# Layered diffusion block on one Trainium2 core: the 31-tap convolution of the conformer's second 128 channels moved from VectorE to TensorE

## The chip, the core and the metric

The kernel runs on one core of one Trainium2 chip. The metric is the device time of one execution in microseconds (us), as the median of several runs. TensorE is called PE here, its weight loads PEld, VectorE DVE, ScalarE ACT, GpSimd POOL; SP is the queue that issues nearly all transfers (DMAs).

## The reference, cut to what matters

There are two layers over 1024 latent and 256 context tokens, 1024 wide. In each layer a normalised stream `h` is projected by `w_in`, four mixers of 256 channels work on parts of the projection, and their outputs go through `w_out` and then a mixture of experts. The third mixer is the conformer:

```
def conformer_conv(pc, conv_w, conv_b, ln_g, ln_b, w_pw, b_pw):
    u = pc[..., :W_C] * jax.nn.sigmoid(pc[..., W_C:])
    u = dwconv(u, conv_w, conv_b, (CONF_K // 2, CONF_K // 2))
    u = layer_norm(u, ln_g, ln_b)
    return jax.nn.silu(u) @ w_pw + b_pw
```

`dwconv` is a depthwise convolution: each of the 256 channels has 31 taps of its own, and runs along the tokens. Latent and context tokens are convolved apart. In the second layer the context produces no mixer output, so the conformer has 1024 tokens there and 1280 in the first.

## The kernel before, in words

A layer runs in four stages: the projection (`phase1`, L2049), the attention inside the same function, a stage that holds the Hyena mixer and the conformer (in `run`, from L2180 on), and the output projection with the experts. Instructions are traced in the order of the code; a planner then lays them out on each engine by readiness and by that order, so that work traced late fills gaps of the engine, and each engine runs its own list strictly in order.

In the projection, `win` (L1070) loads 128 columns of `w_in` at a time, splits them into two parts of reduced precision (ACT at L974, POOL or DVE at L977) and runs three matmul sets at L1091 for every group of 512 or 256 tokens; `win_v` does the like at L1133. Between these blocks lies the recurrence `rglru` (L1403): for each of two channel blocks there are six steps (three stretches, two directions). In a step POOL starts `rg_u` (L1428), three DVE instructions finish it (L1430), PE multiplies it by the gate weights (L1433), and ACT, DVE and POOL go on from there. There is one `rg_u` buffer, so the next step starts only when L1440 of this one is done.

The conformer's input is written by `glu_evac` (L1137): ACT takes a tanh, DVE multiplies at L1147 into the padded row buffer `cu`, one per 128 channels. `conv31` (L1470) is traced at the end of the projection for both channel blocks. It is one DVE instruction at L1475 and 30 at L1477 per block, each over all tokens of the layer (1295 or 1024 elements per partition), accumulating in `cacc`, which is then stored to `cd` in DRAM.

In the later stage `hyena_in` (L1739) loads a row block `hx`, runs L1753 on POOL and two L1756 on DVE, and PE turns the result with matmuls at L1763. `hyena` is a generator: its first part is pulled by `next(hy)`, the rest is traced after the conformer. The long convolution of the Hyena mixer is the matmuls at L1800. `conformer` (L1490) loads the convolved channels back (`cx`, L1499) for 512, 512 and 256 tokens, forms the layer norm through PE (L1502, L1511, L1486), and ends with the product L1524. All of these take PSUM buffers `rg`, of which there are three.

Of the kernel before, what the change touches and what calls it, by code (L numbers as in the profile page):

```python
# [238 lines left out]
FT = mybir.dt.float32  # L239
# [3 lines left out]
AF = mybir.ActivationFunctionType  # L243
OP = mybir.AluOpType
AX = mybir.AxisListType
SP = mybir.EngineType.SP
D = 1024
P = 128
# [629 lines left out]
TL, TC = 1024, 256  # L878
T0 = TL + TC
C8 = math.sqrt(0.5)  # L880
GROUPS = [(0, 512, 0), (512, 512, 0), (1024, 256, 1)]


# [9 lines left out]
class Kern:  # L893
# [22 lines left out]
    def setup(self):  # L916
        nc, I = self.nc, self.I
        moe_consts(self, NFIX)
        c = self.consts
        self.eps = c.tile([P, 2], FT, name="eps")  # L920
        nc.vector.memset(self.eps[:, 0:1], 1e-6)
        nc.vector.memset(self.eps[:, 1:2], 1e-5)
        self.modd = self.dram.tile([2, 2, 6 * D], FT, name="modd")
        self.xd = self.dram.tile([TL, D], FT, name="xd")
        self.x1d = [self.dram.tile([T0 if l == 0 else TL, D], FT, name=f"x1d{l}") for l in range(2)]
        self.pd = self.dram.tile([6 * P, T0], FT, name="pd")
        self.qkd = self.dram.tile([2, 8, 32, 4, T0], FT, name="qkd")
        self.hd = [self.dram.tile([17, P, 512], FT, name=f"hd{l}") for l in range(2)]
        self.hdc = self.dram.tile([5, P, 512], FT, name="hdc")
        self.h2d = [self.dram.tile([T0 if l == 0 else TL, D], FT, name=f"h2d{l}") for l in range(2)]  # L930

        self.fd = [self.dram.tile([2 * T0, D], FT, name="fd0"), self.x1d[1]]
        self.lst = self.dram.tile([64 * P, 4], I32, name="lst")
        self.yd = self.dram.tile([8, P, T0], FT, name="yd")
        self.cd = self.dram.tile([2 * P, T0 + 15], FT, name="cd")

    def params(self, l, psum, R):

# [198 lines left out]
    def glu_evac(self, w, u):  # L1137

        nc, th = self.nc, []

        def f(p, t0, n, v):
            th[:] = [w.tile([P, 512], FT, name="stg", bufs=2)]
            nc.scalar.activation(th[0][:, :n], p[:, :n], AF.Tanh, scale=0.5)

        def g(p, t0, n, v):
            o = t0 + 15 + (15 if v else 0)
            nc.vector.scalar_tensor_tensor(u[:, o:o + n], th[0][:, :n], 1.0, p[:, :n], op0=OP.add, op1=OP.mult)  # L1147
        return f, g

    def d_evac(self, w, row):  # L1150
# [316 lines left out]
        return f  # L1467


    def conv31(self, l, w, b, u, ctx_out):  # L1470
        nc = self.nc
        N = TL + (15 + TC if ctx_out else 0)
        a = w.tile([P, N], FT, name="cacc")
        cw = lambda j: self.cw[:, j * 2 + b:j * 2 + b + 1]
        nc.vector.tensor_scalar(a, u[:, 0:N], cw(0), self.pc("c_conv_b", b), op0=OP.mult, op1=OP.add)  # L1475
        for j in range(1, 31):
            nc.vector.scalar_tensor_tensor(a, u[:, j:j + N], cw(j), a, op0=OP.mult, op1=OP.add)  # L1477
        nc.sync.dma_start(self.cd[b * P:(b + 1) * P, :N], a)

    def spread(self, p, r, t):  # L1480

# [5 lines left out]
        return p  # L1487


    def conformer(self, l, w, ctx_out):  # L1490
        nc, I = self.nc, self.I
        om = w.tile([P, P], FT, name="om", bufs=1)
        nc.vector.memset(om, 1.0 / 256)
        wpw = w.tile([P, 2, 256], FT, name="wpw", bufs=1)
        nc.sync.dma_start(wpw, I["c_w_pw"][l].rearrange("(k p) f -> p k f", p=P))
        for o, t0, n in ((0, 0, 512), (512, 512, 512), (15 + TL, TL, TC))[:3 if ctx_out else 2]:
            acc = w.tile([P, 2, 512], FT, name="cx", bufs=2)
            for b in range(2):
                nc.sync.dma_start(acc[:, b, :n], self.cd[b * P:(b + 1) * P, o:o + n])  # L1499
            pm = self.pr.tile([P, 512], FT, name="rg")  # L1500
            for b in range(2):
                nc.tensor.matmul(pm[:, :n], om, acc[:, b, :n], start=(b == 0), stop=(b == 1))  # L1502
            sq = w.tile([P, 2, 512], FT, name="csq", bufs=1)
            for b in range(2):
                nc.vector.tensor_tensor(acc[:, b, :n], acc[:, b, :n], pm[:, :n], op=OP.subtract)
            nc.scalar.activation(sq[:, :, :n], acc[:, :, :n], AF.Square)

            pv = self.pr.tile([P, 512], FT, name="rg")
            for q in range(n // P):
                for b in range(2):  # L1510
                    nc.tensor.matmul(pv[:, q:q + 1], sq[:, b, q * P:(q + 1) * P], om[:, 0:1], start=(b == 0),  # L1511
                                     stop=(b == 1))
            r = w.tile([P, 4], FT, name="crs", bufs=2)[:, :n // P]
            nc.scalar.activation(r, pv[:, :n // P], AF.Sqrt, bias=self.eps[:, 1:2])
            nc.vector.reciprocal(r, r)
            r = self.spread(self.pr.tile([P, 512], FT, name="rg"), r, w.tile([P, 512], FT, name="cr", bufs=1))
            for b in range(2):
                nc.vector.tensor_tensor(acc[:, b, :n], acc[:, b, :n], r[:, :n], op=OP.mult)
                nc.scalar.activation(acc[:, b, :n], acc[:, b, :n], AF.Silu, scale=self.pc("c_ln_g", b),
                                     bias=self.pc("c_ln_b", b))  # L1520
            for m in range(2):
                p = self.pr.tile([P, 512], FT, name="rg")
                for b in range(2):
                    nc.tensor.matmul(p[:, :n], wpw[:, b, m * P:(m + 1) * P], acc[:, b, :n], start=(b == 0),  # L1524
                                     stop=(b == 1))
                t = w.tile([P, 512], FT, name="cy", bufs=2)
                nc.scalar.activation(t[:, :n], p[:, :n], AF.Identity, bias=self.pc("c_b_pw", m))
                nc.sync.dma_start(self.yd[4 + m, :, t0:t0 + n], t[:, :n])


    def sin_layer(self, w, p, r, n, f, fb, out):
# [517 lines left out]
    def phase1(self, l, ctx_out, top, p1, hs, ahead, done):  # L2049
# [5 lines left out]
        with p1 as c:  # L2055
            with ExitStack() as c2:
# [9 lines left out]
                vt = self.pool(c, "vt").tile([P, 10, 256], FT, name="vt")  # L2066
                wd = self.pool(c, "wd")

                self.cw = self.keep.tile([P, 62], FT, name="cw")
                a = self.col["c_conv_w"]  # L2070
                nc.vector.tensor_scalar(self.cw, self.pp[:, a:a + 62], 0.5, None, op0=OP.mult)
                N = TL + 30 + (15 + TC if ctx_out else 0)
                us = []
                self.pr = self.pool(c2, "r_ps", 3, space=PSUM)
                with ExitStack() as c3:
                    rg = self.pool(c3, "rgl")
# [8 lines left out]
                    def gate(b, h):  # L2085
                        self.win(l, w, [2 + b], hs, allg, [self.rglru_out(wd, b, h)])
                    h = recur(0)
                    for b in range(2):
                        u = wd.tile([P, N], FT, name="cu", bufs=2)
                        nc.gpsimd.memset(u[:, 0:15], 0.0)  # L2090
                        nc.gpsimd.memset(u[:, 15 + TL:30 + TL], 0.0)
                        if ctx_out:
                            nc.gpsimd.memset(u[:, N - 15:N], 0.0)
                        self.win(l, w, [12 + b, 10 + b], hs, allg, self.glu_evac(wd, u))
                        us.append(u)
                    gate(0, h)
                    h = recur(1)
                    with ExitStack() as c4:
# [6 lines left out]
                            if i == 0:  # L2105
                                self.win_v(l, w, wq, hs, vt)
                        gate(1, h)
                for b in range(2):
                    self.conv31(l, wd, b, us[b], ctx_out)
            yt = self.pool(top, f"yt{l}", side="right").tile([P, nblk, 256], FT, name="yt")  # L2110

            def rest(rows):
# [20 lines left out]
    def run(self):  # L2133
# [30 lines left out]
        for l in range(2):  # L2164
# [16 lines left out]
            with ExitStack() as c:  # L2181
                self.pm = self.pool(c, "x_ps", 5, space=PSUM)
                self.pr = self.pool(c, "r_ps", 3, space=PSUM)
                ut = self.pool(top, f"ut{l}", side="right").tile([P, nblk, 768], FT, name="ut")
                hy = self.hyena(l, self.pool(top, f"hy{l}", side="right"), ctx_out, ut, yt)
                with ExitStack() as c2:
                    hc = self.pool(c2, "hc")
                    w = self.pool(c2, "xy")
                    for b in range(2):
                        self.hyena_in(l, hc, b, ut, ctx_out)  # L2190
                    next(hy)
                    self.to_channels(w, yt, 1, nblk)
                    for b in range(2, 6):
                        self.hyena_in(l, hc, b, ut, ctx_out)
                    self.conformer(l, w, ctx_out)
                wop = ExitStack()
                wo = self.pool(wop, "wo")
                with ExitStack() as c2:
                    wo = self.out_weights(l, wo, self.pool(c2, "wor"))
                pin = self.inputs(self.pool(wop, "pi"))  # L2200
                for _ in hy:
                    pass
# [136 lines left out]
```

## Time and profile before

| what | us |
|---|---|
| median of 3 runs (lowest, highest) | 3560.05 (3556.44, 3561.93) |
| the profiled execution's own time | 3566.47 |
| its span, first to last instruction | 3564.7 |
| PE busy, DVE busy in it | 3079.1, 2283.5 |
| the 120 instructions at L1477 | 194.7 |

The span is the profiled execution from its first to its last instruction; 1.8 us of its own time lie around it. Busy times are shares of the whole span and mix stages with different limits, so the rows further down are read stage by stage. A group's mean is over all instructions of that form. Matmul records are pipelined: the time from one start to the next is the pace, and the printed duration is longer. One fp32 matmul of the code is two records.

### The profile page before, as it was taken

To read this page: it belongs to the slowest core of one execution; us is meant where nothing else is said; L and a number is where in the kernel's file an instruction comes from. 1 tells how busy PE (TensorE), PEld (TensorE's weight loads), DVE (VectorE), ACT (ScalarE), POOL (GpSimd) and SP (SyncE) were. 2 spreads that over 40 slices of the span, in tenths; PEclk is the share of its full clock that TensorE was granted. 3 is DMA by queue.
4 is the path that set the end of the run, shared out by engine and by line. 5 is a ranking of instruction groups with operands and counts; after the bars stand their busy time and mean duration, and the time that the engine had idled before them with its cause. 6 is when DMAs were issued, how large, how long until landed. Compare 5 with 4: busy or idle time off the path is not lost. (4 is left out here: it accounts for less than half of the span.)

```text
span 3564.7 us, 43773 instructions
## 1 busy us (share of the span) xinstructions
PE 3079.1 (86%) x14952; PEld 2075.7 (58%) x14952; DVE 2283.5 (64%) x3339; ACT 1539.3 (43%) x2497; POOL 722.9 (20%) x573
## 2 busy tenths in 40 slices
PE   5898888997889699999998487799788799889995
PEld 1246665776678354677555466667667665456563
DVE  6674885787768434475544679578876764347644
ACT  4234344773324233465544354367433343235433
POOL 2213452003210101110110435400230112111110
PEclk8899899998999699999999698989989799999998
DMA  6752226215555888986878512312446389978897
GB/s 189 227 193 62 69 87 215 72 38 178 166 190 195 261 307 320 357 320 237 317 259 333 195 33 101 128 41 70 157 149 228 130 297 361 373 260 280 268 335 252
DMA packets 414223, 734.95 MB, mean 206 GB/s; under 512 B 46725, under 2 KB 181746, under 8 KB 413994
## 3 DMA queue, kind: packets, MB, share of 16 engines
q1 hardware_dynamic: 395242, 694.30, 56.3%
q0 software_dynamic: 18752, 37.80, 3.8%
q8 instruction: 119, 1.95, 0.2%
q14 instruction: 110, 0.90, 0.1%
HBM read 647.75 MB, written 105.30 MB: 211 GB/s over the span
## 5 line engine op out<-in xcount | busy, mean ns | idle before, releaser
L688 DVE TENSOR_TENSOR wl<-wr,wh 128x1024 fp32r<-128x1024 f32 (+1 forms) x440 | 516.0, 1203 | 344.6 <-ACT wh L687 335.7
L687 ACT ACTIVATE wh<-wr 128x1024 fp32r<-128x1024 f32 (+1 forms) x440 | 442.7, 1038 | 391.9 <-PE mm L739 228.7
L743 PE MATMUL mm<-wr,xl 128*64 128x512 f32 x1216 | 329.6, 610 | 6.2 <-DMA wr<-in_moe_w_gate_dram 3.2
L1091 PE MATMUL mm<-hh,wih 128*128 128x512 f32 (+1 forms) x752 | 290.5, 387 | 10.6 <-ACT stg L1155 7.0
L1091 PE MATMUL mm<-hh,wil 128*128 128x512 f32 (+1 forms) x752 | 289.6, 386 | 10.5 <-POOL wil L977 9.9
L1091 PE MATMUL mm<-hl,wih 128*128 128x512 f32 (+1 forms) x752 | 290.9, 387 | 4.4 <-DVE hl L977 3.8
L739 PE MATMUL mm<-wh,xh 128*128 128x512 f32 x704 | 289.6, 413 | 5.1 <-ACT wh L687 4.5
L739 PE MATMUL mm<-wl,xh 128*128 128x512 f32 x704 | 280.0, 398 | 8.4 <-DVE wl L688 8.3
L739 PE MATMUL mm<-wh,xl 128*128 128x512 f32 x704 | 278.6, 397 | 0.0
L1477 DVE SCALAR_TENSOR_TENSOR cacc<-cu,cw,cacc 128x1295 f32<-128x1295 f32 (+1 forms) x120 | 194.7, 1623 | 1.9
L739 PEld LDWEIGHTS mm<-wh,xh 128*128 128x128 f32 x704 | 134.0, 190 | 90.8 <-issue 47.5
L680 POOL DMA_INDIRECT gb<-h2d,ridx x82 | 100.5, 1225 | 420.0 <-PE tr L707 175.9
L1225 DVE TENSOR_REDUCE m<-A 128x1 f32<-128x1024 f32 x128 | 156.2, 1220 | 44.9 <-PE A L1215 36.4
L743 PEld LDWEIGHTS mm<-wr,xl 128*64 128x64 f32 x1216 | 96.5, 137 | 144.3 <-issue 128.1
L977 POOL TENSOR_TENSOR wil<-wir,wih 128x1024 fp32r<-128x1024 f32 x34 | 92.0, 2705 | 426.1 <-ACT wih L974 361.2
L1091 PEld LDWEIGHTS mm<-hh,wih 128*128 128x128 f32 x752 | 146.9, 196 | 40.9 <-ACT stg L1155 10.6
L1091 PEld LDWEIGHTS mm<-hh,wil 128*128 128x128 f32 x752 | 147.5, 196 | 38.9 <-POOL wil L977 10.9
L1091 PEld LDWEIGHTS mm<-hl,wih 128*128 128x128 f32 x752 | 147.2, 196 | 36.1 <-issue 6.6
L810 POOL DMA_INDIRECT x1d<-ot,ridx x40 | 71.1, 1778 | 447.7 <-DVE ot L803 351.4
L789 PE MATMUL mm<-wr,hl 128*64 128x512 f32 x608 | 156.9, 609 | 0.0
L739 PEld LDWEIGHTS mm<-wl,xh 128*128 128x128 f32 x704 | 134.5, 191 | 37.1 <-DVE wl L688 11.3
L1270 ACT ACTIVATE wT<-TR 128x512 f32<-128x512 f32 (+1 forms) x200 | 104.9, 524 | 107.9 <-PE TR L1265 98.7
(489 smaller groups left out, 6530.8 us busy)
## 6 DMA issues: line engine op xcount, KB each, us to landing
wr<-in_moe_w_gate_dram SPq DMA_DIRECT2D x256, 512.0 KB
wr<-in_moe_w_up_dram SPq DMA_DIRECT2D x256, 512.0 KB
wr<-in_moe_w_down_dram SPq DMA_DIRECT2D x256, 512.0 KB
wada<-in_w_ada_dram SPq DMA_DIRECT2D x48, 512.0 KB
tabc<-in_k_t_c_dram SPq DMA_DIRECT2D x88, 256.0 KB
wir<-in_w_in_dram SPq DMA_DIRECT2D x40, 512.0 KB
wr<-in_w_ada_dram SPq DMA_DIRECT2D x32, 512.0 KB
ks<-qkd SPq DMA_DIRECT2D x16, 640.0 KB
```

The source lines that it names most:

```text
L680: self.K.nc.gpsimd.indirect_dma_start(out=g[s, :D // (1 + h)], out_offset=None, in_=self.h2d[h], in_offset=bass.IndirectOffsetOnAxis(ap=id ...
L687: nc.scalar.activation(hi, src, AF.Copy)
L688: nc.vector.tensor_tensor(lo, src, hi.bitcast(FT), op=OP.subtract)
L739: nc.tensor.matmul(ps[b][w], x(k), y[:, kk], start=(k == 0 and c == 0), stop=(k == 7 and c == 2))
L743: nc.tensor.matmul(ps[b][0][w * 64:(w + 1) * 64], self.XT[n0 + b](k), raw[w][:, kk], start=(k == 0), stop=(k == 7))
L789: nc.tensor.matmul(po[b][0][o * 64:(o + 1) * 64], HT[b][:, k], raw[:, o], start=(k == 0), stop=(k == 3))
L810: s = nc.gpsimd.indirect_dma_start(out=self.fd[h], out_offset=bass.IndirectOffsetOnAxis(ap=tidx[r], axis=0), in_=ot[r], in_offset=None, bo ...
L977: (eng or nc.vector).tensor_tensor(lo, src, hi.bitcast(FT), op=OP.subtract)
L1091: nc.tensor.matmul(p[:, :n], a[:, k], b[:, k, t0:t0 + n], start=(k == 0 and a is wh and b is hh), stop=(k == 7 and a is wl))
L1225: nc.vector.tensor_reduce(m[:, c, 1:2], A[c], axis=AX.X, op=OP.max, negate=True)
L1270: nc.scalar.activation(o, i_, AF.Copy)
L1477: nc.vector.scalar_tensor_tensor(a, u[:, j:j + N], cw(j), a, op0=OP.mult, op1=OP.add)
```

## The change

The first 128 channels keep `conv31`. For the second 128 channels `glu_evac` writes its product into the small staging tile and sends it to a padded DRAM buffer `ud`. `taps` gathers the taps by eight small loads, turns them on PE, copies them on ACT, and spreads them on POOL into 64 stationary tiles of 128 rows by 32 columns. `conv31_pe` loads, for a group of tokens, four shifted copies of the input (32 channels by four shifts on the partitions, four channel groups beside one another) and runs 8 x 4 matmuls into the four 32-row parts of one PSUM buffer; ACT adds the bias on the way out. The conformer becomes a generator, so that its first group is traced between the fourth and the fifth `hyena_in`. The modulation loads of the attention still take two `cu` buffers, of which the projection now fills one.

```diff
+UW = T0 + 46
-        self.cd = self.dram.tile([2 * P, T0 + 15], FT, name="cd")
+        self.cd = self.dram.tile([P, T0 + 15], FT, name="cd")
+        self.ud = self.dram.tile([P, UW], FT, name="ud")
+        z = c.tile([P, 16], FT, name="zeros")
+        nc.vector.memset(z, 0.0)
+        for o, n in ((0, 15), (15 + TL, 15), (30 + T0, 16)):
+            nc.sync.dma_start(self.ud[:, o:o + n], z[:, :n])
...
-            nc.vector.scalar_tensor_tensor(u[:, o:o + n], th[0][:, :n], 1.0, p[:, :n], op0=OP.add, op1=OP.mult)
+            t = u[:, o:o + n] if u else th[0][:, :n]
+            nc.vector.scalar_tensor_tensor(t, th[0][:, :n], 1.0, p[:, :n], op0=OP.add, op1=OP.mult)
+            if not u:
+                nc.sync.dma_start(self.ud[:, o:o + n], t)
...
-    def conv31(self, l, w, b, u, ctx_out):
+    def conv31(self, l, w, u, ctx_out):
...
+    def taps(self, l, w):
+        nc = self.nc
+        cw = self.I["c_conv_w"][l]
+        R = w.tile([64, 4, 32], FT, name="taps", bufs=1)
+        nc.gpsimd.memset(R, 0.0)
+        for j in range(8):
+            m = min(4, 31 - 4 * j)
+            nc.sync.dma_start(R[j * 8:(j + 1) * 8, :m],
+                              bass.AP(tensor=cw.tensor, offset=cw.offset + 4 * j * 256, ap=[[32, 8], [256, m], [1, 32]]))
+        p = self.pr.tile([P, 512], FT, name="rg")
+        nc.tensor.transpose(p[:, :64], R.rearrange("r s c -> r (s c)"), self.ident[:64, :64])
+        t = w.tile([P, 64], FT, name="tapsT", bufs=1)
+        nc.scalar.activation(t, p[:, :64], AF.Copy, scale=0.5)
+        one = w.tile([P, 32], FT, name="tap1", bufs=1)
+        nc.vector.tensor_reduce(one, self.ident.rearrange("p (s c) -> p c s", s=4), axis=AX.X, op=OP.add)
+        W = w.tile([P, 64, 32], FT, name="tapw", bufs=1)
+        nc.gpsimd.tensor_tensor(W, one[:, None, :].to_broadcast([P, 64, 32]), t[:, :, None].to_broadcast([P, 64, 32]),
+                                op=OP.mult)
+        return W
+
+    def conv31_pe(self, w, W, out, t0, n):
+        nc, b = self.nc, 1
+        x = w.tile([P, 4, 540], FT, name="cr4", bufs=2)
+        u = self.ud.rearrange("(g c) t -> c g t", g=4)
+        o = t0 + (15 if t0 >= TL else 0)
+        for s in range(4):
+            nc.sync.dma_start(x[s * 32:(s + 1) * 32, :, :n + 28], u[:, :, o + s:o + s + n + 28])
+        p = self.pr.tile([P, 512], FT, name="rg")
+        for j in range(8):
+            for g in range(4):
+                nc.tensor.matmul(p[g * 32:(g + 1) * 32, :n], W[:, j * 8 + b * 4 + g], x[:, g, 4 * j:4 * j + n],
+                                 start=(j == 0), stop=(j == 7))
+        nc.scalar.activation(out, p[:, :n], AF.Identity, bias=self.pc("c_conv_b", b))
...
-            for b in range(2):
-                nc.sync.dma_start(acc[:, b, :n], self.cd[b * P:(b + 1) * P, o:o + n])
+            nc.sync.dma_start(acc[:, 0, :n], self.cd[:, o:o + n])
+            self.conv31_pe(w, W, acc[:, 1, :n], t0, n)
...
+            yield
...
-                for b in range(2):
-                    self.conv31(l, wd, b, us[b], ctx_out)
+                self.conv31(l, wd, u, ctx_out)
...
+                    cm = self.conformer(l, w, ctx_out, self.taps(l, w))
                     self.to_channels(w, yt, 1, nblk)
-                    for b in range(2, 6):
+                    for b in range(2, 4):
                         self.hyena_in(l, hc, b, ut, ctx_out)
-                    self.conformer(l, w, ctx_out)
+                    next(cm)
+                    for b in range(4, 6):
+                        self.hyena_in(l, hc, b, ut, ctx_out)
+                    for _ in cm:
+                        pass
```

## Rows read from the trace of the kernel before

**Rows 1.** The page, part 1: busy time, share of the span, instructions of each engine.
```profile
PE 3079.1 (86%) x14952; PEld 2075.7 (58%) x14952; DVE 2283.5 (64%) x3339; ACT 1539.3 (43%) x2497; POOL 722.9 (20%) x573
```

**Rows 2.** Windows: stretch, busy PE PEld DVE ACT POOL, clock, DMA share, GB/s.
```profile
276.00:337.00 61.00, 52.38 (x237) 40.68 (x236) 21.63 (x33) 28.33 (x39) 17.18 (x25) 0.94 0.21 63
...
415.00:520.00 105.00, 80.81 (x427) 66.43 (x426) 94.26 (x81) 45.28 (x62) 56.22 (x32) 0.87 0.27 92
520.00:567.00 47.00, 46.31 (x239) 39.44 (x238) 20.81 (x23) 15.59 (x23) 27.58 (x16) 1.00 0.51 175
2059.00:2087.00 28.00, 24.89 (x104) 19.08 (x104) 15.52 (x23) 19.71 (x26) 12.81 (x12) 1.00 0.15 41
...
2165.00:2262.00 97.00, 77.95 (x399) 63.54 (x400) 86.62 (x82) 45.72 (x61) 47.70 (x29) 0.85 0.22 76
...
834.00:1020.00 186.00, 138.38 (x593) 112.25 (x594) 138.70 (x175) 49.20 (x74) 70.03 (x76) 0.87 0.57 184
2537.00:2697.00 160.00, 122.39 (x499) 95.61 (x500) 131.13 (x166) 42.16 (x61) 58.57 (x62) 0.85 0.53 167
```

**Rows 3.** DVE groups by form: 415 to 520, then 2165 to 2262.
```profile
L1477 DVE SCALAR_TENSOR_TENSOR cacc<-cu,cw,cacc 128x1295 f32<-128x1295 f32 x30 | 52.5, 1749 | 0.3
...
L1477 DVE SCALAR_TENSOR_TENSOR cacc<-cu,cw,cacc 128x1024 f32<-128x1024 f32 x30 | 43.5, 1451 | 0.4
```

**Rows 4.** PE groups by form, 415 to 520: busy, mean ns, idle before, releaser.
```profile
L1133 PE MATMUL mm<-wvh,hl 128*128 128x256 f32 x80 | 23.9, 298 | 0.0
...
L1091 PE MATMUL mm<-hl,wih 128*128 128x512 f32 x39 | 17.4, 446 | 0.0
...
L1433 PE MATMUL rg<-rg_u,gw 128*128 128x512 f32 x16 | 12.2, 903 | 16.1 <-DVE rg_u L1430 16.1
...
L1091 PE MATMUL mm<-hl,wih 128*128 128x256 f32 x16 | 4.7, 295 | 0.0
L1433 PE MATMUL rg<-rg_u,gw 128*128 128x256 f32 x8 | 4.1, 674 | 8.1 <-DVE rg_u L1430 8.1
```

**Rows 5.** PE waits, 2165 to 2262: total us, times, longest.
```profile
PE rg L1433 <- DVE rg_u L1430: 25.3, 6, 7.4
```

**Rows 6.** PE timeline at full clock: start, us, form, count.
```profile
567.18 0.39 PE L1091 MATMUL mm<-hh,wil 128*128 128x512 f32 x1
567.41 0.39 PE L1091 MATMUL mm<-hh,wih 128*128 128x512 f32 x1
...
571.40 0.27 PE L1091 MATMUL mm<-hh,wil 128*128 128x256 f32 x1
571.51 0.28 PE L1091 MATMUL mm<-hh,wih 128*128 128x256 f32 x1
...
857.12 1.89 PE L1800 MATMUL mm<-z_u,tabc 128*128 128x256 f32 x8
```

**Rows 7.** PE timeline: matmuls of few columns, and one of 128 after them.
```profile
595.57 1.04 PE L1005 MATMUL mm<-cu,sT 128*2 128x256 f32 x14
...
1505.62 3.65 PE L789 MATMUL mm<-wr,hl 128*64 128x512 f32 x16
1509.21 0.50 PE L739 MATMUL mm<-wh,xh 128*128 128x512 f32 x1
```

**Rows 8.** PE timeline of the Hyena stages: idle before, in brackets.
```profile
882.76 2.37 PE L1763 MATMUL rg<-ident,hu 128*128 128x128 f32 x10 [5.75 <-DVE hu L1756]
...
893.72 2.37 PE L1763 MATMUL rg<-ident,hu 128*128 128x128 f32 x10 [5.59 <-DVE hu L1756]
...
2581.33 1.97 PE L1763 MATMUL rg<-ident,hu 128*128 128x128 f32 x8 [6.74 <-DVE hu L1756]
```

**Rows 9.** POOL: a split's min/median/max ns, then a timeline row of the Hyena stage.
```profile
L977 POOL TENSOR_TENSOR wil<-wir,wih x34: 2341/2558/3599, 290.7 to 2454.8; 128x1024 fp32r<-128x1024 f32 x34
...
855.55 1.42 POOL L1753 TENSOR_SCALAR hu<-hx,pp 128x1281 f32<-128x1281 f32 x1 [7.98 <-DMA hx<-pd]
```

**Rows 10.** SP timeline, first issue of the program.
```profile
0.73 0.42 SPq L1564 DMA_DIRECT2D tab<-in_k_feats_l_dram  x1
```

More of the change, by code (lines that the diff above doesn't have):

```diff
@@ L1467, in rglru_out @@
         return f
-    def conv31(self, l, w, b, u, ctx_out):
-        nc = self.nc
+    def conv31(self, l, w, u, ctx_out):
+        nc, b = self.nc, 0
         N = TL + (15 + TC if ctx_out else 0)
         a = w.tile([P, N], FT, name="cacc")
-        cw = lambda j: self.cw[:, j * 2 + b:j * 2 + b + 1]
+        cw = lambda j: self.cw[:, j:j + 1]
         nc.vector.tensor_scalar(a, u[:, 0:N], cw(0), self.pc("c_conv_b", b), op0=OP.mult, op1=OP.add)
@@ L1477, in conv31 @@
             nc.vector.scalar_tensor_tensor(a, u[:, j:j + N], cw(j), a, op0=OP.mult, op1=OP.add)
-        nc.sync.dma_start(self.cd[b * P:(b + 1) * P, :N], a)
+        nc.sync.dma_start(self.cd[:, :N], a)
+    def taps(self, l, w):
[30 more added lines that the diff above has]
+        nc.scalar.activation(out, p[:, :n], AF.Identity, bias=self.pc("c_conv_b", b))
     def spread(self, p, r, t):
@@ L1487, in spread, with conformer @@
         return p
-    def conformer(self, l, w, ctx_out):
+    def conformer(self, l, w, ctx_out, W):
         nc, I = self.nc, self.I
@@ L2067, in phase1 @@
                 wd = self.pool(c, "wd")
-                self.cw = self.keep.tile([P, 62], FT, name="cw")
+                self.cw = self.keep.tile([P, 31], FT, name="cw")
                 a = self.col["c_conv_w"]
-                nc.vector.tensor_scalar(self.cw, self.pp[:, a:a + 62], 0.5, None, op0=OP.mult)
+                nc.vector.tensor_scalar(self.cw, self.pp[:, a:a + 62:2], 0.5, None, op0=OP.mult)
                 N = TL + 30 + (15 + TC if ctx_out else 0)
-                us = []
                 self.pr = self.pool(c2, "r_ps", 3, space=PSUM)
@@ L2087, in phase1 @@
                     h = recur(0)
-                    for b in range(2):
[L2089 to L2095, printed above, removed]
+                    u = wd.tile([P, N], FT, name="cu", bufs=2)
+                    nc.gpsimd.memset(u[:, 0:15], 0.0)
+                    nc.gpsimd.memset(u[:, 15 + TL:30 + TL], 0.0)
+                    if ctx_out:
+                        nc.gpsimd.memset(u[:, N - 15:N], 0.0)
+                    for b in range(2):
+                        self.win(l, w, [12 + b, 10 + b], hs, allg, self.glu_evac(wd, None if b else u))
                     gate(0, h)
```

## Prediction

> **What bounds the kernel now.** The page comes first, to see that no engine's total decides: PE is busy 86% of the span and DVE 64% [rows 1], so the moved convolution counts only where one of them is waited for. Next come the windows over the stretch in which the second convolution runs. From 415 to 520 in layer 0 DVE is busy 94.26 of 105 us and PE 80.81 at a clock of 0.87; from 2165 to 2262 in layer 1 it is 86.62 and 77.95 of 97 us at 0.85. Behind it, from 520 to 567, PE is busy 46.31 of 47 at full clock [rows 2]. So PE sets the end of the projection, and whatever it lost before 520 is added to the time. The groups by form say what DVE does there: 30 instructions of the second block's convolution take 52.5 us in layer 0 and 43.5 in layer 1 [rows 3]. PE's own groups and waits say what it loses: before the gate matmuls L1433 it idles 16.1 + 8.1 = 24.2 us on DVE's `rg_u` in layer 0 [rows 4] and 25.3 us in layer 1 [rows 5]. DVE works strictly in order, so each of the six recurrence steps stands behind convolution instructions, and PE, also in order, stands at L1433 with ready projection matmuls behind it.
>
> How much of the stretch is lost? At full clock one record of 512 columns starts 0.23 after the one before, one of 256 columns 0.12 at most, and eight fp32 records of 256 take 1.89, or 0.24 each (0.47 at 512) [rows 6]. The work from 415 to 520 is 240 records at L1133 (three sets of 80), 48 at L1091 of 256 columns (three of 16), 115 of 512 (39, and two sets of 38), and the gates' 16 and 8 [rows 4]: 288 x 0.12 + 115 x 0.23 + 16 x 0.47 + 8 x 0.24 = 70.5 us. So 34.5 of 105 us are lost, 24.2 to the named wait and some 10 to the lower clock and small breaks. In layer 1 I add 5 to the 25.3, an estimate from its shorter busy time: 30.
>
> **What the removal gives.** Two stretches of the same recurrence run before any convolution competes: 276 to 337 (four steps) and 2059 to 2087 (three). PE idles 61 - 52.38 = 8.6 us in the first and 28 - 24.89 = 3.1 in the second, all waits counted, or 2.2 and 1.0 us a step, at clocks of 0.94 and 1.00 [rows 2]. With the convolution it is 24.2 / 6 = 4.0 and 25.3 / 6 = 4.2. I take 1.6 a step as what stays, 10 us per layer, since POOL still feeds `rg_u` and its weight splits of at least 2.3 us [rows 9] stay in front of it. That returns 14 + 15 = 29 us of idle time, and I take 10 of the 15 us of clock and breaks, as the clock was higher wherever PE waited less. **Gain 39.** Upper bound: 1.0 a step and the whole rest, 18 + 19 + 15 = 52. Lower bound, while DVE was the limit: 2.2 a step and no clock, 11 + 12 = 23. The first block's convolution stays where it is and ends near 415, so it covers and costs what it did.
>
> **What is added, part by part.**
> - Start: three stores of zeros come first on SP, whose first issue takes 0.42 us [rows 10], and wait for a memset. Its queue runs back to back there: 2 us, between 0 and 4.
> - `glu_evac`: the DVE product is the same size; five small stores go onto SP and hold the staging tile until they land. SP also waits for POOL's splits, so a store can stand behind a weight load by up to two splits of 2.3 to 3.6 us [rows 9]. 1 us, between 0 and 8.
> - Convolution on PE: 32 matmuls a group, 64 records. Two tiles of 64 columns ran 16 fp32 records of 512 columns in the 3.59 us to the next matmul, 0.22 each [rows 7], half of 0.47: the two run beside one another. With four tiles of 32 columns I take half again, 0.11, so 7 us for 512 tokens and 3.5 for 256. The nearest row for four parts is the modulation's 14 records of 256 columns in 1.04, 0.074 each with the tail, doubled 0.15 for 512, so 9.5 us a group at most at full clock. I take 7, because that row's tail weighs on only 14 records. Layer 0: 17.5; layer 1: 14; 31.5 together.
> - What covers it: in the Hyena stages PE is busy 138.38 of 186 and 122.39 of 160 us [rows 2], and while DVE finishes the `hyena_in` it waits 5.75 and 5.59 us in layer 0 and 6.74 in layer 1 [rows 8]. The first group of each layer is traced right there and fits: 14 us hidden. If `hyena_in` were not late, these 14 us would show. The other groups (7 + 3.5 and 7) come ahead of the rest of the Hyena in trace order and push it: 17.5 us exposed, between 0 (all in the 85 us of idle PE) and 63 (none, at half clock).
> - Taps: the POOL product writes 2048 elements a partition, twice a split's 1024, so twice 2.4 us; POOL is idle 7.98 us before the third `hyena_in` [rows 9], and behind the product stands that `hyena_in`. 2 us for the pair of layers, between 0 and 10. The eight small loads, a transpose, a copy and a reduce lie beside the first `hyena_in`: nothing, or one more such wait if they land late.
> - Shifted loads: 4 x 540 fp32 on 128 partitions is 1.1 MB for 512 tokens. 184 GB/s at a share of 0.57 [rows 2] is 323 GB/s when busy, so 3.4 us; some 15 us of transfer for 5 MB in both layers, in stages with the share half free. SP stands still for none of it, but the tables and `hx` queue behind. 4 us, between 0 and 15.
>
> **Sum** against the profiled execution's 3566.47: -39 + 2 + 1 + 17.5 + 2 + 4 = -12.5, or 3554. That execution is 6.4 above the median, so for the median 3560.05 - 12.5 = 3547.5, given as 3547. With all bounds together it runs from -50 to +77. Attention, experts and the end keep their work and shift.
>
> [...] A matmul of 128 columns after 16 of 64 starts 3.59 us after their first [rows 7], where 15 starts at half the pace 0.47 and one more tail explain it within some 0.4 us. [...]
>
> **Rivals.**
> - *The convolution hides wholly.* The 85 us of idle PE take the 31.5 us. For it: waits on DVE in both stages [rows 8]. Against it: trace order puts later groups ahead of the Hyena chain. Costs fall to 5 and the gain may come near 45: 3520.
> - *The wait only changes its name.* PE waits at L1433 for a step that also needs POOL, whose splits and rope products stay. If 3 us a step stay and the clock does not recover, the gain is 6 + 7 + a few, some 18, and the 26.5 of costs give about 3567; with half the costs hidden, 3555. For it: POOL is busy 56 of 105 us [rows 2]; against it: the two stretches without convolution, whose POOL work was lighter.
> - *Slower: PE stands at the first shifted load.* Place: the first convolution matmul of a group, with Hyena matmuls queued behind it in order. Price: 5 us for each of five groups while 1.1 MB arrive, and the 31.5 us of matmuls exposed, some of them at half clock: 26.5 + 25 + 10 = 61 against 39, so 3582. It decides once a load lands more than about 3 us after PE reaches it. For it: at 0.57 the transfers take 3.4 us alone and share with the tables. Against it: two buffers, and data that lies ready since the projection. [...]
> - *Four tiles do not run beside one another.* 64 x 0.47 = 30 us a group, 135 in all: about 3650. The 0.074 [rows 7] speaks against it; I leave it 2 in 100.
>
> **How the numbers follow.** About 0.2% (7 us) is what a measurement can tell from no change: below 3553 is faster, above 3567 slower. My forecast has 0.45, most of it below 3553 (0.33) and some within (0.10); hidden wholly 0.20, all faster; the renamed wait 0.20, of which 0.07 faster, 0.10 within and 0.03 slower; slower by the loads 0.15 with the tiles' 0.02 in it, 0.13 of it slower and 0.02 within. That gives 0.60, 0.22 and 0.18. The range runs from 3516, just past the hidden case, to 3574, past the renamed wait and short of the loads' full price.
>
> **What would show it.** Right: L1477 in 60 instructions; PE's wait for `rg_u` after the first convolution under 12 us a layer and the clock there above 0.92; 320 records of 128 x 32 starting 0.11 apart; each Hyena stage some 10 us longer; SP's first load about 2 us later. Wrong: an `rg_u` wait that stays above 18 a layer, with POOL as DVE's releaser (renamed wait); PE idle on the tile `cr4` for over 3 us a group (loads); starts 0.4 apart (no tiles); Hyena stages no longer than before (hidden). The prediction fails if the projection after the first convolution shrinks by less than 10 us a layer.

## The result, and the profile after

The changed kernel takes 3603.9 us (median of 4 runs, 3596.2 to 3610.2) against 3558.2 us before in the same runs: ratio 1.0123, 95% interval 1.0108 to 1.0138, so 38 to 49 us **slower**. The forecast was 3547 with a range up to 3574. The profiled execution took 3610.15 us, its span is 3608.3.

The page, part 1, of the kernel after; [rows 1] answer to it:

```profile
PE 3097.4 (86%) x15274; PEld 2077.2 (58%) x15274; DVE 2189.1 (61%) x3280; ACT 1542.8 (43%) x2504; POOL 695.5 (19%) x572
```

DVE lost 94.4 us of work and PE gained only 18.3, with 322 instructions more; the sums look like a good trade. Where the time went is read by laying the two timelines over one another: the same instruction (same line, operands and turn) is looked up in both profiled executions and its start subtracted, and the median of a short stretch is taken.

| place (time before, us) | shift after minus before, us |
|---|---|
| first recurrence steps, layer 0 (276) | +3.6 |
| end of the attention, layer 0 (812) | -9.2 |
| first output product, layer 0 (1021) | +30.9 |
| before the recurrence, layer 1 (2058) | +24.6 |
| end of the attention, layer 1 (2530) | +10.5 |
| first output product, layer 1 (2694) | +43.8 |
| end (3560) | +43.7 |

The projections gain 13 and 14 us, as the change means them to. Each stage with the Hyena and the conformer loses more: 40.1 us in layer 0 and 33.3 in layer 1. These two numbers are what has to be explained.

**Projection.** The windows of the stretch of [rows 2] in the kernel after (columns as there), then PE's longest wait in it, layer 0 and layer 1 (us in total, times, longest):

```profile
419.00:520.00 101.00, 83.08 (x454) 69.14 (x454) 50.32 (x57) 47.77 (x66) 49.43 (x36) 0.92 0.28 96
...
2189.00:2278.00 89.00, 72.99 (x401) 60.79 (x402) 48.77 (x56) 46.17 (x62) 43.86 (x32) 0.91 0.24 83
```
```profile
PE rg L1443 <- DVE rg_u L1440: 17.9, 6, 4.8
...
PE rg L1443 <- DVE rg_u L1440: 21.8, 6, 7.6
```

DVE is now busy half the time, and PE still waits 17.9 and 21.8 us for `rg_u` where [rows 4] and [rows 5] had 24.2 and 25.3. DVE's own waits there (layer 0) point to the reason: it stands in the recurrence's chain, behind ACT and POOL.

```profile
DVE rg_i L1445 <- ACT rg_i L1444: 13.8, 5, 3.7
DVE rg_t L1450 <- POOL rg_u L1448: 11.6, 5, 2.7
...
DVE rg_u L1440 <- POOL rg_u L1438: 8.0, 4, 3.3
```

**Convolution on PE.** The instructions of its matmul line (duration in ns: least, median, most; first and last start), and who waited:

```profile
L1527 PE MATMUL rg<-cr,tapw x320: 379/592/617, 882.4 to 2631.6; 128*32 128x512 f32 x128, 128*32 128x256 f32 x32
...
  DMA cr<-ud: 0.7, 1
```

PE waited 0.7 us in all for a shifted load. The groups are in the timeline of PE, here the stretch of layer 0 around them (start, duration; in brackets the idle time before and its releaser):

```profile
882.39 7.07 PE L1527 MATMUL rg<-cr,tapw 128*32 128x512 f32 x64 [0.68 <-DMA cr<-ud]
889.39 1.99 PE L1554 MATMUL rg<-cx,om 128*128 128x512 f32 x4
899.41 3.57 PE L1563 MATMUL rg<-om,csq 128*128 128x1 f32 x16 [8.03 <-ACT csq L1558]
904.37 2.05 PE L1537 MATMUL rg<-cr,ones_f 128*128 128x512 f32 x2 [1.38 <-DVE cr L1534]
909.38 6.54 PE L1576 MATMUL rg<-cx,wpw 128*128 128x512 f32 x8 [2.96 <-ACT cx L1571]
915.76 2.79 PE L1816 MATMUL rg<-ident,hu 128*128 128x128 f32 x20
918.53 7.07 PE L1527 MATMUL rg<-cr,tapw 128*32 128x512 f32 x64
925.53 2.00 PE L1554 MATMUL rg<-cx,om 128*128 128x512 f32 x4
927.38 2.75 PE L1853 MATMUL mm<-Yl,tabc 128*128 128x256 f32 x12
...
943.09 3.66 PE L1527 MATMUL rg<-cr,tapw 128*32 128x256 f32 x64
...
974.53 2.93 PE L1853 MATMUL mm<-z_x,tabc 128*128 128x256 f32 x6 [10.11 <-DVE z_x L1764]
```

In the kernel before, the same chain of the first group had the inverse transform (L1800 on `Yl`) in between, and the butterfly on `z_x` came with hardly a wait:

```profile
908.16 1.95 PE L1511 MATMUL rg<-om,csq 128*128 128x1 f32 x16
...
913.07 3.19 PE L1800 MATMUL mm<-Yl,tabc 128*128 128x256 f32 x14
...
950.34 1.56 PE L1800 MATMUL mm<-z_x,tabc 128*128 128x256 f32 x6 [1.18 <-DVE z_x L1711]
```

The reader is to see three things. A group takes 7.07 us for 512 tokens. The conformer's first group then runs almost alone on PE, which idles 8.03, 1.38 and 2.96 us in its layer norm chain. And the Hyena's inverse transform (L1853 on `Yl`) starts only at 927.38, behind the second group, so that at its own end nothing is left to cover the butterfly: 10.11 us on `z_x`. In layer 1 the like waits are 9.6 us on `csq` and 20.3 on `z_x`. The clock was low behind these four waits, 0.50 in the matmuls that followed each (899.4 to 903.0, 974.5 to 977.4, 2609.6 to 2613.2, 2678.6 to 2680.6): behind the 8.03 us of idle time the 16 matmuls on `csq` took 3.57 us; the second group's 16, from 930.0 on, took 1.95 us at 1.00.

The stages in windows: from the last transposition of the attention to the first output product, first the kernel before, then after (columns as in [rows 2], PE first):

```profile
823.80:1020.80 197.00, 148.38 (x646) 120.47 (x647) 146.93 (x187) 51.52 (x79) 70.10 (x76) 0.88 0.55 177
2536.30:2694.40 158.10, 120.12 (x493) 93.65 (x494) 131.83 (x166) 42.16 (x61) 58.57 (x62) 0.86 0.53 168
```
```profile
814.60:1051.70 237.10, 174.93 (x841) 129.84 (x841) 146.18 (x188) 53.15 (x83) 68.67 (x78) 0.85 0.51 157
2546.80:2738.20 191.40, 135.09 (x622) 99.63 (x623) 133.74 (x166) 43.52 (x64) 58.12 (x63) 0.83 0.49 150
```

PE's busy time grows by 26.6 and 15.0 us (the convolution is 17.8 and 14.1 of that; of the other 8.8 us in layer 0 the stretches at 0.50 are a part, with 1.6 on `csq`: 3.57 where the kernel before had 1.95), and its idle time by 13.5 and 18.3 (237.1 - 174.9 against 197.0 - 148.4, and so on).

### The profile page after: what moved, and what is told of

Same layout as the page of the kernel before. It is cut to its first block, busy times and chain, and to the rows that moved or that the text cites. A ratio compares the mean times of both kernels' runs of the same rounds, so it can differ in the third digit from the quotient of the medians.

```text
span 3608.3 us, 44465 instructions
## 1 busy us (share of the span) xinstructions
PE 3097.4 (86%) x15274; PEld 2077.2 (58%) x15274; DVE 2189.1 (61%) x3280; ACT 1542.8 (43%) x2504; POOL 695.5 (19%) x572
## 3 DMA queue, kind: packets, MB, share of 16 engines
q1 hardware_dynamic: 398890, 698.20, 56.3%
## 5 line engine op out<-in xcount | busy, mean ns | idle before, releaser
L984 POOL TENSOR_TENSOR wil<-wir,wih 128x1024 fp32r<-128x1024 f32 x34 | 90.2, 2653 | 428.5 <-ACT wih L981 359.4
L739 PEld LDWEIGHTS mm<-wl,xh 128*128 128x128 f32 x704 | 134.1, 191 | 36.2 <-DVE wl L688 11.1
L739 PEld LDWEIGHTS mm<-wh,xl 128*128 128x128 f32 x704 | 133.7, 190 | 28.8
```

Source lines behind the costliest of these rows:

```text
L739: nc.tensor.matmul(ps[b][w], x(k), y[:, kk], start=(k == 0 and c == 0), stop=(k == 7 and c == 2))
L984: (eng or nc.vector).tensor_tensor(lo, src, hi.bitcast(FT), op=OP.subtract)
```

## The experiments

The first four kernels ask which part of the 73 us of the stages belongs to what. The first theory was that of the **cover**: the early first group, traced between two `hyena_in`, has nothing beside it. Its rival was the **work** itself.

**Order of before.** `hyena_in` 2 to 5 first, then the conformer whole:
```diff
-for b in range(2, 4): self.hyena_in(...)
-next(cm)
-for b in range(4, 6): self.hyena_in(...)
+for b in range(2, 6): self.hyena_in(...)
```


> The conformer is traced as before, whole, after the sixth hyena_in; the convolution on PE stays. Cover theory (the early first group leaves its layer norm chain without other PE work, PE idle grew by 13 us in the first stage and 19 in the second): most of these 32 us come back, about 3578 us, and PE's wait for csq falls from 8.0 and 9.6 to under 2. Work theory (the stages are longer by the convolution's matmuls and what they push, the order of tracing has no part in it): 3600 to 3610, or up to 3615 if the early group had been hidden under hyena_in.

Measured: 3613.0 us, 1.0144 [1.0127, 1.0161]. The first theory fell in this form: with the order of before nothing came back. The 7 us by which it is slower than the change (1.0144 - 1.0123, times 3560) are within the two intervals.

**Convolution left out, with the change's order and with the order of before.**
```diff
-self.conv31_pe(w, W, acc[:, 1, :n], t0, n)
+nc.sync.dma_start(acc[:, 1, :n], self.cd[:, o:o + n])
```
(and no `taps`; the second kernel also has the edit above).

> No taps, no shifted loads, no convolution matmuls: the second half of cx is loaded from the first block's result, so the convolution of the second block is left out; the early first group stays. Cover theory: the idle that the early group makes stays, some 3604 - 32 of matmuls = 3572. Work theory: everything the stages gained in length goes, 3604 - 71 = 3533.

> As the run before, and the conformer traced as in the kernel before: what is left of the change is the shorter work on DVE in the projection, the small stores and the zero stores. Both theories: the projections' gain of 13.3 and 14.0 less 3.6 at the start, so 3558 - 24 = 3534. If the stages are longer even so, the stores into ud or the planner's new order cost something there.

Measured: 3538.3 us, 0.9935 [0.9917, 0.9953], and 3540.0 us, 0.9933 [0.9910, 0.9956]. So the shorter work on DVE is worth 23 us (16 to 32), and all of it is kept when nothing is put on PE. The stages take 199.4 and 158.8 us in the first, as before (197.0 and 158.1): neither the stores nor the order alone cost anything.

**One block of taps instead of eight.** Loads, taps product and order stay.
```diff
-for j in range(8):
+for j in range(1):
```


> The convolution group runs 4 matmuls instead of 32 (one block of four taps, the others are left out); taps, shifted loads and the order stay. Work theory: 7/8 of 31.8 us of matmuls go and what they push, 3570 to 3576. Cover theory: the same matmuls go but the idle stays or grows, 3576 to 3585. Loads or POOL product theory (1.1 MB a group and 4.1 us in front of the third hyena_in hold the stage): 3590 or more.

Measured: 3707.9 us, far outside. 122 us of it come between 1980 and 2000, in the experts of layer 0 (PE waits 92.0 us on a load of `xg` that it doesn't wait for otherwise). Which tokens go to which expert depends on the values, and these differ here; that this is the cause is not shown. The total says nothing then, but the stages do:

```profile
811.60:1039.20 227.60, 161.75 (x673) 124.36 (x673) 149.28 (x188) 53.49 (x83) 67.77 (x78) 0.81 0.53 163
2654.80:2838.50 183.70, 122.39 (x510) 94.16 (x511) 133.75 (x166) 43.28 (x64) 59.48 (x63) 0.80 0.51 156
```

Seven eighths of the matmuls are gone (27.9 us) and the stages are 9.5 and 7.7 us shorter, 17 in all; idle grew by 3.7 and 5.0. They are still 53 us longer than without convolution (411.3 against 358.2). So the **matmuls' own time is the smaller part** of the 73. That left taps, loads, queues and order.

**Taps without convolution.** The edit of `cx` as above, but `taps` stays:
```diff
-self.conv31_pe(w, W, acc[:, 1, :n], t0, n)
+nc.sync.dma_start(acc[:, 1, :n], self.cd[:, o:o + n])
```


> The taps are built as in the change, but no shifted loads and no convolution matmuls: the second half of cx is loaded from the first block's result (the second block's convolution is left out). Without the taps this stood at 3538. Taps theory (eight loads on SP, the transpose on PE and the 4.1 us product on POOL in front of the third hyena_in are most of the 20 us a stage that the matmuls don't explain): 3565 or more. Loads theory (the shifted loads and SP's order behind them are): 3540 to 3548.

Measured: 3553.0 us, 0.9974 [0.9960, 0.9988]: 14 us above the kernel without them (0.9974 - 0.9935, times 3560), between the two theories. The stages are 208.8 and 161.6 us long, so 9.4 us fall into layer 0. Not a small term.

**SP's waits.** In the kernel after SP stands 22.4 us at a store of `cy` and has the inverse's tables behind it:

```profile
SPq L1580 <- ACT cy L1579: 28.6, 6, 22.4
```
```diff
-nc.sync.dma_start(self.yd[4 + m, :, t0:t0 + n], t[:, :n])
+nc.scalar.dma_start(self.yd[4 + m, :, t0:t0 + n], t[:, :n])
```


> The change, with the conformer's output stores cy issued by ACT, which makes cy, instead of SP. Queue theory (SP stands 22.4 and 19.1 us at the first group's cy stores with the inverse's tables and H loads behind them, and PE begins the inverse 9 us after they are issued): SP's wait goes and 8 to 18 us a stage come back, 3570 to 3588. Chain theory (PE idles on the layer norm's chain and the next butterfly, whatever SP does): 3600 to 3606, and the tables land early without being used.

Measured: 3601.4 us, 1.0109 [1.0088, 1.0129]: nothing. SP now stood 21.1 us at the third group's load of `cx`, which waits for a buffer. So the next kernel also had:
```diff
-x = w.tile([P, 4, 540], FT, name="cr4", bufs=2)
+x = w.tile([P, 4, 540], FT, name="cr4", bufs=3)
...
-acc = w.tile([P, 2, 512], FT, name="cx", bufs=2)
+acc = w.tile([P, 2, 512], FT, name="cx", bufs=3)
```


> The change with the conformer's loads cx and cr4 in three buffers instead of two and its stores cy issued by ACT: the same 20 shifted loads stay on SP, but none of SP's conformer instructions waits for a buffer or for cy any more. Queue theory (what costs is SP standing at such a wait with the inverse's tables behind it): 3570 to 3582, near the run with the loads on POOL's queue (3573). Rival (the number of issues on SP, and the order that comes of it, costs without any wait): 3595 to 3606.

Measured: 3603.2 us, 1.0122 [1.0088, 1.0157]: nothing again, and the traces say why. SP's timeline, then PE's:

```profile
901.26 2.16 SPq L1743 DMA_DIRECT2D tabc<-in_k_t_c_dram  x4
903.79 0.33 SPq L1743 DMA_DIRECT2D tab<-in_k_t_s_dram  x1
```
```profile
904.52 3.57 PE L1563 MATMUL rg<-om,csq 128*128 128x1 f32 x16 [8.48 <-ACT csq L1558]
909.47 2.05 PE L1537 MATMUL rg<-cr,ones_f 128*128 128x512 f32 x2 [1.38 <-DVE cr L1534]
914.48 6.53 PE L1576 MATMUL rg<-cx,wpw 128*128 128x512 f32 x8 [2.96 <-ACT cx L1571]
...
923.62 7.07 PE L1527 MATMUL rg<-cr,tapw 128*32 128x512 f32 x64
...
932.46 2.75 PE L1853 MATMUL mm<-Yl,tabc 128*128 128x256 f32 x12
```

The inverse's tables are issued at 901.26, and in the kernel after at 917.52; PE comes to the inverse at 932.46, 31 us later, because its list has the conformer's chain, the transpositions and the second group ahead of it. At this place not a queue holds the inverse back but the **order of PE's list**. (SP is not wholly free here: after these tables it stands 16.9 us for a store of `cy` to land.)

**Loads on POOL's queue.**
```diff
-nc.sync.dma_start(x[s * 32:(s + 1) * 32, :, :n + 28], ...)
+nc.gpsimd.dma_start(x[s * 32:(s + 1) * 32, :, :n + 28], ...)
```


> The change, with the shifted loads cr4 issued from POOL's queue instead of SP. Loads theory (20 issues in SP's order and their waits for a free buffer hold the tables and hx): 15 to 30 us come back, 3575 to 3590. If the bytes or PE's chain hold the stage and not the queue: 3600 to 3606. If POOL's own time for the descriptors delays hu: over 3610.

Measured: 3573.2 us, 1.0030 [1.0018, 1.0043]: some 33 us back (1.0123 - 1.0030, times 3560). The number fits the loads theory, but PE's timeline shows the other cause at work as well. In layer 0 the inverse is spread through the first group's chain, and the wait for `csq` is gone (in layer 1 it is 5.6 us, after 9.6):

```profile
889.19 0.65 PE L1853 MATMUL mm<-Yl,tabc 128*128 128x256 f32 x2
...
892.84 7.07 PE L1527 MATMUL rg<-cr,tapw 128*32 128x512 f32 x64
...
901.69 1.89 PE L1853 MATMUL mm<-Yl,tabc 128*128 128x256 f32 x8
903.41 1.03 PE L1853 MATMUL mm<-Ysum,tabc 128*128 128x256 f32 x4
904.32 1.95 PE L1563 MATMUL rg<-om,csq 128*128 128x1 f32 x16
```

Then the zero stores and tap loads on POOL's queue too, and half the product:
```diff
-nc.sync.dma_start(self.ud[:, o:o + n], z[:, :n])
+nc.gpsimd.dma_start(self.ud[:, o:o + n], z[:, :n])
...
-W = w.tile([P, 64, 32], FT, name="tapw", bufs=1)
+W = w.tile([P, 32, 32], FT, name="tapw", bufs=1)
```


> The loads on POOL's queue as before, and with them the zero stores at the start and the eight tap loads; the taps' product writes only the 32 tiles that are used. Sum of the parts: 3.6 us at the start and about 5 of the taps come back from 3573: 3562 to 3567, still not under the kernel before. If POOL's issue time delays hu or the start: 3573 or more.

Measured: 3571.1 us, 1.0044 [1.0028, 1.0060]: no further gain. The shift at 240 us is 7.9 there, and 0.7 to 9.4 in the eleven kernels with the zero stores on SP, so the 3.6 after is not a price of these stores.

**Order alone.** To part order from load, the loads went back to SP, and the Hyena's second part (inverse and second forward transform) was traced ahead of the rest of the conformer:
```diff
+next(hy)
 for _ in cm:
     pass
```


> The change, with one edit: the second part of the Hyena generator (the first inverse transform and the second forward one) is traced before the rest of the conformer, not behind it; the 20 shifted loads stay on SP. Order theory (in the change PE's list holds the first group's layer norm chain, 20 transposes and the second group's convolution ahead of the inverse, and PE idles in that chain and again at the next butterfly): 20 to 30 us come back, 3574 to 3584. Load theory (loads on SP cost by themselves, the tables arrive behind them in any order): 3598 to 3606.

Measured: 3579.8 us, 1.0054 [1.0037, 1.0070]. This is the order theory's number: 25 us back, 0.69% of 3560, with all 20 loads on SP. The windows of the stages and PE's timeline:

```profile
810.40:1024.00 213.60, 169.07 (x839) 126.41 (x840) 146.85 (x188) 53.10 (x83) 65.98 (x78) 0.87 0.56 172
2520.10:2695.90 175.80, 136.92 (x622) 101.08 (x623) 132.89 (x166) 43.18 (x64) 57.71 (x63) 0.85 0.52 161
```
```profile
877.79 7.07 PE L1527 MATMUL rg<-cr,tapw 128*32 128x512 f32 x64 [0.56 <-ACT ut L1817]
884.80 1.99 PE L1554 MATMUL rg<-cx,om 128*128 128x512 f32 x4
886.63 2.75 PE L1853 MATMUL mm<-Yl,tabc 128*128 128x256 f32 x12
895.23 3.57 PE L1563 MATMUL rg<-om,csq 128*128 128x1 f32 x16 [5.85 <-ACT csq L1558]
...
928.15 7.07 PE L1527 MATMUL rg<-cr,tapw 128*32 128x512 f32 x64
...
937.76 1.13 PE L1853 MATMUL mm<-z_x,tabc 128*128 128x256 f32 x4 [0.60 <-DVE z_x L1764]
```

The inverse starts at 886.63, and the second group covers the butterfly: 0.60 us where it was 10.11. The stages are 23.5 and 15.6 us shorter than after. (This profiled execution, 3565.3, is the shortest of nine, so part of these 39 us is its own; the medians give 25.)

PE's time in the two stages, layer 0 and layer 1, in the four kernels that matter (us; the last three rows are parts of the idle time):

| | before | no convolution, order of the change | after | order alone |
|---|---|---|---|---|
| length | 197.0, 158.1 | 199.4, 158.8 | 237.1, 191.4 | 213.6, 175.8 |
| busy | 148.4, 120.1 | 147.7, 118.1 | 174.9, 135.1 | 169.1, 136.9 |
| idle | 48.6, 38.0 | 51.7, 40.7 | 62.2, 56.3 | 44.5, 38.9 |
| waits on `hu` (`hyena_in`) | 25.5, 13.8 | 17.2, 6.2 | 11.6, 6.2 | 11.1, 6.0 |
| waits on `csq` | 0.6, 1.9 | 1.2, 6.6 | 8.0, 9.6 | 7.3, 7.5 |
| waits on `z_x` (L1764, before: L1711) | 1.2, none | 8.5, 0.3 | 12.9, 23.7 | 3.4, 3.8 |

The new order takes away the waits on `z_x`, not those on `csq`. With it PE idles about as long as in the kernel before, and the added matmuls come on top of that.

The same line on top of the kernel with the small transfers on POOL's queue, and in the kernel before, ahead of its whole conformer:
```diff
+next(hy)
 self.conformer(l, w, ctx_out)
```


> The same reordering on top of the run with all the change's small transfers on POOL's queue (3571). If order and queue are two ways to the same 30 us: 3565 to 3573. If they add: 3540 to 3555, under the kernel before.

> The kernel before with the same reordering and no other edit, as a control. In the kernel before the planner already interleaves the inverse with the conformer, so no change is expected: 3553 to 3563. If it is faster by 10 or more, what the reordering gives belongs to the Hyena and not to the moved convolution.

Measured: 3565.7 us, 1.0015 [1.0000, 1.0030], and 3552.8 us, 0.9977 [0.9959, 0.9996]. Queue and order don't add up: together 38 us come back by the ratios, where the queue alone gave 28 (the 3571.1 above) and the order 25. The control is 8 us faster than the kernel before (1 to 15), the only kernel here with the whole convolution that beats both; by the timelines 7 us of it fall into the stage of layer 0 and hardly any into that of layer 1. So some 8 of the 25 us of the order are the Hyena's own, and would be had without the change.

**Other places for the same convolution.** On PE in the projection, traced behind the first block's:
```diff
 self.conv31(l, wd, u, ctx_out)
+W = self.taps(l, wd, N - 30)
+for t0 in range(0, T0 if ctx_out else TL, 256):
+    self.conv31_pe(wd, W, X, t0 + (15 if t0 >= TL else 0), t0, 256)
```


> The second block's convolution stays on PE but runs in the projection, traced behind the first block's, in groups of 256 tokens; its result goes to DRAM as before and the conformer is as in the kernel before. Cover theory (PE still idles 17.9 and 21.8 us on rg_u there, and the Hyena stage has no free chain): some 5 to 10 of the 32 us of matmuls show, 3545 to 3555, under both kernels. Rival (PE is full behind 520, and the shifted loads come too late for the gaps): all 32 show, 3570 or more.

Measured: 3623.9 us, 1.0174 [1.0156, 1.0191]. The groups ran from 558 to 614 in layer 0, behind the gaps at 415 to 520: with one buffer and the tap loads issued at 548, PE waited 7.8 us for the taps and 11.4 for the input.

On DVE, but later:
```diff
-for b in range(2): self.conv31(l, wd, b, us[b], ctx_out)
+self.conv31(l, wd, 0, us[0], ctx_out)
...
+with self.tc.issue_after(self.begun[0]):
+    self.conv31(l, wd, 1, us[1], ctx_out)
```


> The kernel before, with the second block's convolution left on DVE but issued after the attention has begun. DVE is busy 203 of 267 us there and PE 246, so 52 us fit into its idle time on paper: 3540 to 3550 if they do. Rival (PE waits for DVE in the attention as it did in the projection): the gain is given back, 3555 to 3570.

Measured: 3558.7 us, 1.0013 [0.9994, 1.0033]. The edit did not move the work (it still ran between 414 and 520 in layer 0), so this tells nothing of the attention.

On POOL, a product and a sum per tap: first traced behind the attention, then held back by a dependency on the attention's output, then with its store on POOL's queue, last with the Hyena's reordering. The core of it:
```diff
+for j in range(1, 31):
+    nc.gpsimd.tensor_scalar(q[:, :n], u[:, o + j:o + j + n], cw(j), None, op0=OP.mult)
+    nc.gpsimd.tensor_tensor(a[:, o:o + n], a[:, o:o + n], q[:, :n], op=OP.add)
```


> The kernel before, with the second block's convolution on POOL instead of DVE (a product and a sum per tap, 61 instructions for each stretch of tokens), traced behind the attention's start; nothing on PE. POOL idles some 250 of 267 us in the first attention stage. Cover theory: the projections gain their 22 to 27 us and nothing else moves: 3533 to 3543. Rival (POOL's work slows DVE beside it, or holds the modulation's buffers in the attention): 3550 or more.

> The kernel before, with the second block's convolution on POOL, in pieces of 256 tokens, and held until the attention's first output exists by a true dependency (its taps are rewritten with an operand from there); the modulation's loads in the first layer use one buffer instead of three. POOL needs about 5.3 us a tap and 1024 tokens, some 200 us in the first layer, of about 230 that are left of the attention there, and 160 in the second. Cover theory: the projections' 22 to 27 us come back, 3533 to 3543. Rival (POOL's end comes late, or DVE slows beside it): 3550 to 3600.

> As pool_attn, with POOL's result stored from POOL's own queue instead of SP, pieces of 341 and 342 tokens, and the start tied to the attention's first exponential. POOL's rows give 0.41 + 2.38 per 1000 elements for a product and 0.22 + 2.10 for a sum: some 248 us in the first layer, of 253 that are left, and 194 in the second, of 225. Cover theory: the projections' 22 to 25 us come back and nothing else moves: 3534 to 3542. Rival (POOL ends late, or the Hyena's POOL work stands behind it): 3550 to 3580.

> The run before with the second part of the Hyena generator traced ahead of the conformer, which gave 8 us on the kernel before. If the two add: 3526 to 3534. If the reordering only covers what POOL's late end opens: the same as the run before.

Measured: 3827.7, 3854.8, 3782.4 and 3773.1 us. In the first the planner put the work into the projection, ahead of the weight splits: 2.97 + 2.39 us a tap for 1024 tokens. In the next two SP's waits name the price, the second and third kernel in turn:

```profile
SPq L1497 <- POOL cacc L1495: 137.4, 1, 137.4
```
```profile
SPq L1078 <- POOL wil L977: 139.9, 3, 128.5
```

SP stands 137.4 us at the store of POOL's result, or 128.5 us at a weight load whose buffer POOL's split behind the convolution still holds, and the attention's loads stand behind SP. Until then the projection of layer 0 had gained 10 us in the third kernel. POOL's idle time is there, the lists in order spoil it.

## Why the prediction was wrong, point by point

**The step that failed** is "What covers it": "The first group of each layer is traced right there and fits: 14 us hidden", with 17.5 us exposed, 2 for the taps and 4 for the loads. The place was right: PE's waits on `hu` fell from 25.5 to 11.6 us and from 13.8 to 6.2. But the idle time did not shrink by that. The waits on `csq` and `z_x` grew by 7.4 and 11.7 us in layer 0 and by 7.7 and 23.7 in layer 1. Against the kernel without convolution the stages are 70 us longer (428.5 against 358.2, both layers): 32 are the convolution's own matmuls, 12 are the other matmuls, the same but for two records, which took longer, in part in the stretches at a clock of 0.50, and 26 are added idle time. I counted PE's idle time as room, but the added matmuls rearranged which waits are covered by what. On balance nothing was hidden, and new idle came beside it.

By the medians the parts are: 23 gained (convolution left out), 42 for the convolution, its taps and loads with the better order (1.0054 - 0.9935), and 25 for the order (1.0123 - 1.0054), of which some 8 are the Hyena's own; -23 + 42 + 25 = +44, where I had -39 + 26.5. The gain is 16 short, the cost 40 over.

- **Bound and mechanism of the gain: right, size too high.** "Gain 39" was 26.9 by the table above (12.8 + 14.1) and 23 by the kernel without convolution, at the lower bound of 23. Of the wait I let 1.6 us a step stay; 3.0 and 3.6 stayed, 17.9 and 21.8 in all against the sign of under 12. The rival of the renamed wait had 3 a step, for POOL's part in it; DVE's waits for POOL and ACT point that way. Why the early stretches had 1.0 to 2.2 a step is open: from 2059 to 2087 DVE, ACT and POOL were busy 55, 70 and 46% [rows 2], as much as here (55, 52 and 49% from 2189 to 2278). The clock came to 0.92 and 0.91.
- **Start 2, `glu_evac` 1:** the shift is 1.9 at 10 to 30 us (0.2 and 0.3 in the two kernels with the zero stores on POOL's queue), and gone at 60; what comes later differs from run to run. The stores add nothing: the shift is 3.6 at 276 and 3.6 at 415.
- **Pace of the convolution: right.** 7.07 us for 512 tokens and 3.66 for 256 against 7 and 3.5; 17.8 + 14.1 us in all. In the timeline no other matmul stands within a group. The rival "four tiles do not run beside one another" is out.
- **Taps 2, at most 10:** 14 (6 to 22) by the kernel that has them alone. POOL's product took 4.1 us, near the estimate of 4.8; that loads, transpose and copy lie "beside the first `hyena_in`" for nothing can't hold then, but which of them ends last was not parted.
- **Loads 4:** moved off SP they gave 33 us back, but 25 come back with them on SP by the order alone. What they cost beside the order is not parted further, and no run shows the 4.
- **The rival on the slow side** came nearest in time (3582) by a cause that was wrong: PE stood 0.7 us at the loads, not 25.
- **Two sums** were slightly off: all lower bounds together give -52, not -50, and the renamed wait with all costs 3569, not 3567. Neither moves the range.

What stays open: why the layout puts the inverse behind the second group when the loads are on SP. The planner's costs are in no trace. Shown is that two edits that bring the inverse forward give 25 and 33 us back, and that two that change SP's waits do not. No run changed the clock by itself, so its share is not parted from that of the waits.

## What to carry to other kernels

Idle time of an engine is not room as long as its list is in order: before counting added work as hidden, name for each wait in the stage which work covers it now, and ask whether it still comes ahead after the change. An addition of 32 us of matmuls cost 67 with its taps and loads, because it displaced the work that covered two other chains; one line of tracing order gave 25 of that back. And work taken off a busy engine returns only what its own chain doesn't hold: the bound to trust was the wait that stays when that engine is idle (here 3.0 and 3.6 us a step with DVE busy half the time).

## What the runs showed of the hardware

- The four column tiles start together: four records within 0.05 us, and each four 0.43 to 0.45 us after the four before at 512 columns, 0.21 to 0.24 at 256.
- The four shifted loads of one group, 1.1 MB in pieces of 2160 bytes, took 7.1 us from first to last piece in layer 0 (889.1 to 896.2) where I had worked out 3.4 from [rows 2]. Some 0.6 MB of other transfers passed in the same 7.1 us; what made the loads take longer than worked out is not shown. It cost nothing, as this data was there before PE asked (the group starts at 918.53).
- PE's granted clock was 1.00 through the first group's convolution (882.4 to 889.4), and 0.50 in the matmuls that followed 8.03 us of idle time; 16 on `csq` took 3.57 us there, and the second group's 16 took 1.95 at 1.00. The half clock that the prediction reckons with is in the trace of the kernel before: 0.50 from 900.0 to 904.0, and the four L1502 matmuls that start at 902.06 took 3.17 us, where the next group's four took 1.88 at 1.00.
- On POOL a product of 128x1024 with one factor per partition took 2.97 us and a sum of two tensors of that size 2.39, so a tap costs 5.4 us; DVE does tap and sum for 1295 tokens in 1.75 [rows 3].
